# The recurrence of block 2: the two heads of a pair in opposite halves of the array

## The chip, the core and the metric

The kernel runs on one core of a Trainium2 chip. The metric is the device time of one execution in microseconds. Five engines work beside each other: TensorE (PE in the profile, its weight loads PEld), VectorE (DVE), ScalarE (ACT), GpSimd (POOL) and SyncE (SP), which issues most DMAs. TensorE's 128x128 array is addressed by rows (the partitions of the two operands) and columns (the partitions of the output in PSUM), so that a matmul with 64 partitions in and 64 out uses one corner of it.

## The reference

Two blocks of two layers each over 512 tokens and 1024 channels. The change lies in the mixer of the second block, an RWKV-7 time mix with 8 heads of 64 channels:

```
for l in range(2):                                   # second block
    h = rms_norm(x) * (1 + sc1) + sh1
    p = h @ w_in                                     # r, k, v, low ranks, pool features, gates
    ps = z + (prev(z) - z) * mu                      # token shift, z = shifted part of p
    decay, a, g = functions of low-rank products
    kk = k * k_k / ||k * k_k||;  k = k * (1 + (a - 1) * k_a)
    # per head and token:  S = S (diag(w) - kk^T (a kk)) + v k^T ;  y = S r
    y = group_norm(y) * lnx_g + lnx_b + (sum r k r_k) v;  y_a = y * g
    y_b = (trailing means over 2, 4, 8, 16 frames - frame) @ pool_w * pool_scale
    x = x + gt1 * ((gate0 * (y_a @ proj_a) + gate1 * (y_b @ proj_b)) @ w_out)
    x = x + gt2 * ffn(x)
```

## The kernel before

**Projections.** Activations lie with channels on partitions, tokens along the free axis (128 x 512 tiles). A projection (lin_steps, L474) forms an output of 128 channels from 8 input tiles; weights and inputs are split into a high and a low part, so each input tile costs three matmuls with 512 columns (L490). Weight units come by DMA on SP's queue (`raw`); ScalarE casts the high part (`wh`, L432) and VectorE, or GpSimd where `fine` is given, subtracts to get the low part (`wl`, L433). With `fine=2` the generator yields after each two input tiles, that is after six matmuls: a step.

**Interleaving.** `together` takes several generators in turn, one step each; `lent(gen, n)` lends n steps of one. The order so written is a priority: the framework plans each engine's own order from it with its cost model, and adds the semaphores. Pools have fixed numbers of buffers; PSUM has two banks for `lin`, three for `ch` and three for `T2`.

**The mixer of block 2 (mix2, L1306).** First the low-rank features (2s), then k and r (2k, 2r), beside which Rwkv.prep makes, for each of four pairs of heads, the scaled keys `bk` and the queries `ar`: the log decay, its sum over each chunk of 64 tokens, the norm of the keys (n2, an rsqrt on VectorE, spread over channels by the transposes Rn) and the products. Then the following steps, in chunks of 64 tokens, 8 per layer, two chunks to a pair:

- `invert` forms for each chunk and head the 128x128 product of keys and queries (`am`, L1620), masks it (`ah`, L1623), gathers all the 32x32 diagonal blocks in one tile (L1625), and inverts them all by 30 dependent rounds of products and sums on VectorE (L1639, L1642). Beside it runs the projection of v (2v), whose evacuation shifts v and adds the bonus (L1599).
- `ready(Q)` puts the inverses back (L1659), makes the off-diagonal block (px, p2) and the transposed, decayed keys (b2 on ScalarE, bt by transposes).
- `chain(Q)` is the recurrence for two chunks one after the other: R = queries times the state plus the part within the chunk (L1713, L1717), up = the inverse times R (L1728), sn = the state's increment (L1738), yp = the output (L1752, L1756), at the end group norm and transposes back. Both heads of a pair use the same rows and the same columns of the array in R and up; the state is a block-diagonal 128x128 tile per pair, so products with it have 128 rows.

Steps of the pool branch (2p) and of a gate (2g1) fill up: 16 steps of 2v beside `invert`, then 5 and 3 around the first `ready`, 12 beside each of the first three pairs of chunks; the last pair runs beside the projection 2pr1. After it come the other gate, 2pr0 and 2out, and the feed-forward part.

Of the kernel before, what the change touches and what calls it, by code (L numbers as in the profile page):

```python
# [16 lines left out]
S = 512  # L17
# [293 lines left out]
def kernel(ctx: ExitStack, tc: tile.TileContext, aps: dict, out: bass.AP, taps=None, stop=None,  # L311
# [162 lines left out]
    def lin_steps(key, mts, hs, evac, first=0, last=0, tag="lin", fine=0):  # L474
# [8 lines left out]
        def fetch(m, tag):  # L483
            if m // gm not in units:
                units[m // gm] = wunit(key, m // gm, tag, G.tensor_tensor if fine or begun and m < 2 else None)
# [117 lines left out]
    def rms_finish(sl, twice=False):  # L603
# [3 lines left out]
        for t in range(4 if twice else 2):  # L607
            o = sl.start + t % 2 * 128
            mm = T.matmul(ms[:, t:t + 1], sums[t // 2][:, o:o + 128], C("ones", 0, 1), start=True, stop=True)
# [696 lines left out]
    def mix2(l):  # L1306
# [22 lines left out]
        ss, rr, kf = [], [], []  # L1329
        lin_fm(("2s", l), 3, hs, shift_ev(ss, 12, "ss", "f"), first=3)  # L1330
# [5 lines left out]
        wsm = {}  # L1336
# [23 lines left out]
        def kr():  # L1360
            wsm.update({n: small(n, l, "f") for n in ("wa2", "gv")})
            yield from lin_steps(("2k", l), 4, hs, shift_ev(kf, 4, "kf", "f"), fine=2)
            yield from lin_steps(("2r", l), 4, hs, shift_ev(rr, 0, "rr", "f"), fine=2)
# [8 lines left out]
        yb = []  # L1372

        def ev_p(g, ps):
            win = PW[g]
            z = U("z", "v")
            A.copy(z, ps)
            cs = U("cs", "v")
# [7 lines left out]
            def project():  # L1386
                p2 = MX("p2")
                T.matmul(p2, pwt[:, g * 128:g * 128 + 128], d, start=True, stop=True)
                t = U("yb2", "f")
                A.copy(t, p2)  # L1390
                yb.append(t)

            soon.append(project)
# [6 lines left out]
        def ev_g1(m, ps):  # L1400
            gt1.append(U("gt1", "bk"))
# [6 lines left out]
        def beside():  # L1408
            yield from lin_steps(("2p", l), 4, hs, ev_p, fine=2)
            tap(f"2yb{l}", yb)  # L1410
            for n, st in enumerate(lin_steps(("2g1", l), 8, hs, ev_g1, fine=2)):
                yield
                if n % 2 and len(yhl1) < 4 <= n // 6:
                    i = len(yhl1)
                    yhl1.append(split(yb[i], "y", "f", psc[:, i:i + 1]))
# [5 lines left out]
        fill = beside()  # L1421
# [7 lines left out]
        run_soon()  # L1429
# [6 lines left out]
        together(rw.chain(NQ - 1), lin_steps(("2pr1", l), 8, yhl1, ev_b1, fine=2))  # L1436
# [33 lines left out]
        def halve(m):  # L1470
            mhl.append(split(merged[m], "m", "bk", 0.5, "ar"))
# [29 lines left out]
    class Rwkv:  # L1501
# [3 lines left out]
        def __init__(self, l, ss, rr, kf, vf, y, lora, hb):  # L1505
# [7 lines left out]
            self.AH, self.BKT = {}, {}  # L1513
            self.st = None

        def prep(self, p):

            l, ss, kf, lora, hb, NC = self.l, self.ss, self.kf, self.lora, self.hb, self.NC
            ps = lora("wup", ss[0], p)
# [4 lines left out]
            V.tensor_tensor_scan(Lc, C("cs"), lw, 0.0, op0=ALU.mult, op1=ALU.add)  # L1524
            yield
            ps = lora("aup", ss[0], p)
            a = U("a", "f")
            A.activation(a, ps, ACTF.Tanh, bias=hb[:, 4 + p:5 + p], scale=0.5)
# [10 lines left out]
            yield  # L1539
            yield  # L1540
            rb = U("rnb", "f", (128, 8, 64))
            A.copy(rb, rn.unsqueeze(2).to_broadcast([128, 8, 64]))
            yield
# [20 lines left out]
            for q in range(2):  # L1564
                hs_ = slice(q * 256, q * 256 + 256)
                bk = U("bk", "bk", (128, 4, 2, 64))
                V.scalar_tensor_tensor(bk[:, :, 0], c4(a[:, hs_]), 0.5, c4(Wi[:, hs_]), op0=ALU.mult, op1=ALU.mult)
                V.tensor_mul(bk[:, :, 1], c4(k2[:, hs_]), c4(Wi[:, hs_]))
# [14 lines left out]
        def bonus(self, p):  # L1583

            l, vf = self.l, self.vf
            bp = MX("bp", "ch")
            T.matmul(bp, C("bones"), self.rr[p], start=True, stop=True)
            if l:
# [5 lines left out]
                V.tensor_sub(dv, dv, vf[p])  # L1594
# [4 lines left out]
            V.tensor_mul(self.y[p], vf[p], bp)  # L1599
            A.activation(self.y[p], self.y[p], ACTF.Identity, bias=VC("lb", l)[:, p:p + 1])  # L1600

        def begin(self):

            self.sbd = [t.rearrange("p (q h v) -> p q h v", q=4, h=2) for t in sums]
            self.swd = U("swd", "f", (128, 4, 64))
            for t in self.sbd:
                G.memset(t.rearrange("p q h v -> p (q h v)"), 0.0)

        def invert(self):

# [4 lines left out]
            for c in range(NC):  # L1615
                for h in range(2):
                    am = c4(MX("am", "T2"))
                    r = slice(64 * h, 64 * h + 64)
                    for p in range(4):
                        T.matmul(am[:, p], BK[2 * p + c // 4][r, c % 4].rearrange("p s t -> p (s t)"),  # L1620
                                 AR[2 * p + c // 4][r, c % 4].rearrange("p s t -> p (s t)"), start=True, stop=True)
                    ah = self.AH[c, h] = U("ah", "f", (128, 4, 128))
                    V.tensor_mul(ah, am, msk("mA"))  # L1623
                    for e in range(2):
                        A.activation(src[64 * h + 32 * e:64 * h + 32 * e + 32, :, 4 * c:4 * c + 4],  # L1625
                                     ah[32 * e:32 * e + 32, :, 32 * e:32 * e + 32].rearrange("s p t -> s t p"),
                                     ACTF.Copy, scale=-1.0)
# [19 lines left out]
        def ready(self, Q):  # L1647

            BK, wc = self.BK, self.wc
# [3 lines left out]
            up, lo = slice(0, 32), slice(32, 64)  # L1653
            four = [(2 * e + h, self.AH[2 * Q + e, h]) for e in range(2) for h in range(2)]
            for n, (i, ah) in enumerate(four):
                c, h = 2 * Q + n // 2, n % 2
                for e in range(2):
                    cp_ = (A.copy, V.tensor_copy, G.tensor_copy)[(2 * n + e) % 3]
                    cp_(ah[32 * e:32 * e + 32, :, 32 * e:32 * e + 32].rearrange("s p t -> s t p"),  # L1659
                        self.inv[64 * h + 32 * e:64 * h + 32 * e + 32, :, 4 * c:4 * c + 4])  # L1660
            yield
            for i, ah in four:
                V.transpose(tn[up, 4 * i:4 * i + 4], ah[up, :, up])
            yield
            for i, ah in four:
                for p in range(4):
                    T.matmul(px[lo, 4 * i + p], ah[up, p, lo], tn[up, 4 * i + p], start=True, stop=True)  # L1667
            A.copy(X[lo], px[lo])
            yield
            for e in range(2):  # L1670
                c = 2 * Q + e
                bt = c4(MX("bt", "T2"))
                b2 = U("b2", "f", (128, 4, 128))
# [10 lines left out]
            for i, ah in four:  # L1684
                for p in range(4):
                    T.matmul(p2[up, 4 * i + p], X[lo, 4 * i + p], ah[lo, p, lo], start=True, stop=True)  # L1686
# [168 lines left out]
```

## Time and profile before

| | us |
|---|---|
| median of 3 runs | 3695.94 (3693.49 to 3697.94) |
| profiled execution, its own time | 3699.74 |
| its span, first to last instruction | 3697.9 |
| PE busy | 3612.5 (98%) |
| DVE busy | 2129.7 (58%) |
| ACT busy | 1501.6 (41%) |
| POOL busy | 719.2 (19%) |

Ends of matmuls are modelled and consecutive ones overlap in the records, so the cadence is read from start to start. Layer 0 of block 2 runs from about 2040 us, layer 1 from about 2860. The granted clock is TensorE's, 1 for 2.4 GHz; the other level is 1.2 GHz.

### The profile page before, as it was taken

What the parts mean: (1) busy time and instruction counts of PE and PEld (TensorE: products, weight loads), DVE (VectorE), ACT (ScalarE), POOL (GpSimd) and SP (SyncE); (2) the same over time, 40 slices, a digit from 0 to 9 for tenths busy, and PEclk for the clock granted to TensorE, in tenths of its full rate; (3) what the DMA queues carried; (4) which work ended last, traced back from release to release, by engine and by line L of the source; (5) the groups of instructions that cost most, each with busy time, mean ns of one, the idle gap of its engine ahead of it and who ended that gap; (6) DMA issues with size and microseconds to landing.
All of it is one profiled execution on the core that took longest, in us unless ns stands there. A gap on an engine that the chain in (4) does not pass through costs nothing. (4 is left out here: it accounts for less than half of the span.)

```text
span 3697.9 us, 48423 instructions
## 1 busy us (share of the span) xinstructions
PE 3612.5 (98%) x17936; PEld 2856.9 (77%) x17936; DVE 2129.7 (58%) x4610; ACT 1501.6 (41%) x2850; POOL 719.2 (19%) x589
## 2 busy tenths in 40 slices
PE   7999999999999999999999889999999999999998
PEld 6667789888876677898888767788888667788887
DVE  6854536667668555366766873364445773363445
ACT  4565524333345545343334553333233543343233
POOL 3523311000044233110000431320000421320000
PEclk9999999999999999999999999999999989999999
DMA  4212322455422123225553221222223111322222
GB/s 136 88 46 69 101 93 98 154 166 188 143 89 84 45 69 103 97 92 165 178 169 132 80 66 41 90 97 92 91 97 114 66 52 41 96 91 97 91 97 75
DMA packets 124894, 367.60 MB, mean 99 GB/s; under 512 B 14704, under 2 KB 19056, under 8 KB 124656
## 3 DMA queue, kind: packets, MB, share of 16 engines
q1 hardware_dynamic: 119264, 357.15, 29.3%
q10 hardware_dynamic: 5392, 7.35, 0.8%
q8 instruction: 141, 2.31, 0.3%
q14 instruction: 97, 0.79, 0.1%
HBM read 350.28 MB, written 7.34 MB: 97 GB/s over the span
## 5 line engine op out<-in xcount | busy, mean ns | idle before, releaser
L432 ACT CAST wh<-raw 128x512 fp32r<-128x512 f32 x1096 | 670.2, 619 | 1532.7 <-PE lnt L490 1444.3
L490 PE MATMUL lnt<-hH,wh 128*128 128x512 f32 (+1 forms) x3184 | 1267.2, 399 | 10.2 <-DVE x L1321 7.2
L490 PE MATMUL lnt<-hL,wh 128*128 128x512 f32 (+1 forms) x3184 | 1233.5, 388 | 2.2 <-DVE hL L643 2.2
L490 PE MATMUL lnt<-hH,wl 128*128 128x512 f32 (+1 forms) x3184 | 1231.2, 387 | 0.0
L433 DVE TENSOR_TENSOR wl<-raw,wh 128x512 fp32r<-128x512 f32 x772 | 537.1, 704 | 643.4 <-ACT wh L432 640.6
L433 POOL TENSOR_TENSOR wl<-raw,wh 128x512 fp32r<-128x512 f32 x324 | 441.8, 1367 | 1601.5 <-ACT wh L432 1568.0
L490 PEld LDWEIGHTS lnt<-hH,wh 128*128 128x128 f32 x3184 | 604.2, 190 | 184.3 <-issue 47.9
L490 PEld LDWEIGHTS lnt<-hL,wh 128*128 128x128 f32 x3184 | 605.8, 190 | 131.0 <-issue 11.5
L490 PEld LDWEIGHTS lnt<-hH,wl 128*128 128x128 f32 x3184 | 604.9, 190 | 130.5 <-issue 3.2
L490 PE MATMUL lnt<-fH,wh 128*128 128x512 f32 (+1 forms) x864 | 313.9, 364 | 0.0
L490 PE MATMUL lnt<-fL,wh 128*128 128x512 f32 (+1 forms) x864 | 313.2, 363 | 0.1
L490 PE MATMUL lnt<-fH,wl 128*128 128x512 f32 (+1 forms) x864 | 312.7, 362 | 0.0
L490 PEld LDWEIGHTS lnt<-fL,wh 128*128 128x128 f32 x864 | 163.2, 189 | 28.5 <-DVE fL L408 0.5
L490 PEld LDWEIGHTS lnt<-fH,wh 128*128 128x128 f32 x864 | 163.2, 189 | 28.2
L490 PEld LDWEIGHTS lnt<-fH,wl 128*128 128x128 f32 x864 | 163.2, 189 | 27.7
L590 POOL TENSOR_TENSOR sums<-sums,sq 128x256 f32<-128x256 f32 (+1 forms) x61 | 53.4, 881 | 563.3 <-ACT sq L588 562.1
L1300 DVE SCALAR_TENSOR_TENSOR x<-lnt,mod,x 128x512 f32<-128x512 f32 (+1 forms) x136 | 88.7, 655 | 92.1 <-PE lnt L490 91.9
L695 DVE SCALAR_TENSOR_TENSOR cv<-lnt,vec,cv 128x511 f32<-128x511 f32 (+1 forms) x168 | 123.9, 744 | 14.7 <-ACT cv L693 13.2
L490 PE MATMUL lnt<-yH,wh 128*128 128x512 f32 x320 | 129.9, 406 | 0.0
L490 PE MATMUL lnt<-yH,wl 128*128 128x512 f32 x320 | 127.6, 399 | 0.0
L490 PE MATMUL lnt<-yL,wh 128*128 128x512 f32 x320 | 126.4, 395 | 0.0
L1281 DVE CUSTOM_DVE_ANT_0 adaw<-adaw,csilu 128x512 f32<-128x512 f32 x192 | 124.5, 685 | 0.0
(389 smaller groups left out, 4330.6 us busy)
## 6 DMA issues: line engine op xcount, KB each, us to landing
raw<-in_wst_dram SPq DMA_DIRECT2D x548, 512.0 KB, 3.3
adaw<-in_ada_dram SPq DMA_DIRECT2D x192, 256.0 KB, 3.5
sw<-rq ACTq DMA_DIRECT2D x96, 64.0 KB, 2.0
xd<-x SPq DMA_DIRECT2D x16, 256.0 KB, 2.5
x<-xd SPq DMA_DIRECT2D x16, 256.0 KB, 3.3
x<-in_xT_dram SPq DMA_DIRECT2D x8, 256.0 KB, 5.8
out_dram<-x SPq DMA_DIRECT2D x8, 256.0 KB, 2.2
csilu<-in_c_dram SPq DMA_DIRECT2D x4, 256.0 KB, 4.4
```

What stands on the lines that cost most here:

```text
L432: A.copy(h[:, :q], raw[:, sl])
L433: sub(l[:, :q], raw[:, sl], h[:, :q].bitcast(F32), op=ALU.subtract)
L490: mm = T.matmul(ps[:, sl], w_, h_[:, sl], start=(k == 0 and i == 0), stop=(k == kt - 1 and i == 2))
L590: G.tensor_tensor(acc[:, sl], acc[:, sl], sq[:, sl], op=ALU.add)
L695: V.scalar_tensor_tensor(y[:, d:], ps[:, :S - d], taps_w[nt - 1 - d], y[:, d:], op0=ALU.mult, op1=ALU.add)
L1281: V.tensor_tensor_reduce(out=w, in0=w, in1=t, scale=1.0, scalar=0.0, op0=ALU.mult, op1=ALU.add, accum_out=sm[:, i:i + 1])
L1300: return V.scalar_tensor_tensor(x[m][:, sl], ps[:, sl], md[:, o + m:o + m + 1], x[m][:, sl], op0=ALU.mult, op1=ALU.add)
```

## The change

In `invert` the am products of two heads alternate and go to two banks. In `ready` each head's blocks stay in its own half of the partitions, and the keys are transposed without the decay. In `chain` the state has no zero halves (128 x 4 x 64), R and up run with head 0 in one half of rows and columns and head 1 in the other, R's part within the chunk is formed for both chunks ahead (R1), the decay is multiplied into the state after the sum, and y is formed for both chunks at the end, into one bank per head. The last transposes and the addition to y become `tail`, which runs beside the next pair. The evacuation of v and the bonus moves from VectorE to ScalarE (both scalings, the copy of the bonus) and GpSimd (sum, products). 2v, 2p and 2g1 become one filler; 31 of its steps run beside `invert`, 5 beside the first `ready`, 9 beside each pair. The pool branch's scan and product come later by a count of matmuls. Besides: the two low-rank products of prep are issued together, the rsqrt of the norms gets more rounds, half of bk goes to GpSimd, the k, r and v projections take banks of `lin` and `T2` in turn, two small weights are fetched earlier, and in rms_finish the sum-of-squares matmuls are tied behind the last projection matmul. The cut core of the diff (of `chain` mainly the new lines):

```diff
 def fetch(m, tag):            # lin_steps
-  ... G.tensor_tensor if fine or begun and m < 2 else None)
+  ... G.tensor_tensor if fine else None)
-            ps = MX("lnt", tag)
+            ps = MX("lnt", tag if isinstance(tag, str) else tag[m % len(tag)])
...
+        with behind() if newest else ExitStack():          # rms_finish
             for t in range(4 if twice else 2):
                 mm = T.matmul(ms[:, t:t + 1], sums[t // 2][:, o:o + 128], C("ones", 0, 1), start=True, stop=True)
...
+        begun.append(smalls)                               # mix2
         lin_fm(("2s", l), 3, hs, shift_ev(ss, 12, "ss", "f"), first=3)
...
+            banks = ("lin", "lin", "T2")
+            yield from lin_steps(("2k", l), 4, hs, shift_ev(kf, 4, "kf", "f"), tag=banks, fine=2)
+            yield from lin_steps(("2r", l), 4, hs, shift_ev(rr, 0, "rr", "f"), tag=banks, fine=2)
...
         def ev_vf(m, ps):
-            shift(vf[m], ps, 8 + m)
+            A.activation(vf[m], ps, ACTF.Identity, bias=0.0, scale=om[:, 8 + m:9 + m])
+            A.activation(t, ps, ACTF.Identity, bias=0.0, scale=mu[:, 8 + m:9 + m])
+            G.tensor_tensor(vf[m][:, 1:], vf[m][:, 1:], t[:, :S - 1], op=ALU.add)
...
+            later.append([20, lambda: pool(g)])            # ev_p
...
+            later.insert(0, [14, project])                 # pool
...
         def beside():
+            yield from lin_steps(("2v", l), 4, hs, ev_vf, tag=("lin", "T2"), fine=2)
             yield from lin_steps(("2p", l), 4, hs, ev_p, fine=2)
...
-        together(rw.invert(), lin_steps(("2v", l), 4, hs, ev_vf, fine=2))
+        together(rw.invert(), lent(fill, 31))
...
-        for _ in lent(fill, 5):
-            pass
-        together(rw.ready(0), lent(fill, 3))
+        together(rw.ready(0), lent(fill, 5))
         for Q in range(NQ - 1):
-            together(rw.chain(Q), rw.ready(Q + 1), lent(fill, 12))
+            together(tails(), rw.chain(Q), rw.ready(Q + 1), lent(fill, 9))
...
+            ps, ps2 = lora("wup", ss[0], p), lora("aup", ss[0], p)      # prep
...
-            yield
-            yield
+            for _ in range(3):
+                yield
             rb = U("rnb", "f", (128, 8, 64))
             A.copy(rb, rn.unsqueeze(2).to_broadcast([128, 8, 64]))
+            yield
             yield
...
-                V.scalar_tensor_tensor(bk[:, :, 0], c4(a[:, hs_]), 0.5, c4(Wi[:, hs_]), op0=ALU.mult, op1=ALU.mult)
-                V.tensor_mul(bk[:, :, 1], c4(k2[:, hs_]), c4(Wi[:, hs_]))
+                for h in range(2):
+                    r = slice(64 * h, 64 * h + 64)
+                    V.scalar_tensor_tensor(bk[r, :, h], c4(a[r, hs_]), 0.5, c4(Wi[r, hs_]), op0=ALU.mult, op1=ALU.mult)
+                    G.tensor_tensor(bk[r, :, 1 - h], c4(k2[r, hs_]), c4(Wi[r, hs_]), op=ALU.mult)
...
+            A.copy(y[p], bp)                                # bonus
-                V.tensor_sub(dv, dv, vf[p])
+                G.tensor_tensor(dv, dv, vf[p], op=ALU.subtract)
-            V.tensor_mul(self.y[p], vf[p], bp)
+            G.tensor_tensor(y[p], y[p], vf[p], op=ALU.mult)
...
-            for t in self.sbd:                              # begin
-                G.memset(t.rearrange("p q h v -> p (q h v)"), 0.0)
...
+                ams = [c4(MX("am", "T2")) for _ in range(2)]            # invert
+                for p in range(4):
+                    for h in range(2):
+                        r = slice(64 * h, 64 * h + 64)
+                        T.matmul(ams[h][:, p], BK[2 * p + c // 4][r, c % 4].rearrange("p s t -> p (s t)"),
+                                 AR[2 * p + c // 4][r, c % 4].rearrange("p s t -> p (s t)"), start=True, stop=True)
...
-                    A.activation(b2[:, p], BK[2 * p + c // 4][:, c % 4].rearrange("p s t -> p (s t)"), ACTF.Copy,
-                                 scale=wc[:, c, p:p + 1])               # ready
-                    T.transpose(bt[:, p], b2[:, p], ident)
+                    T.transpose(bt[:, p], BK[2 * p + c // 4][:, c % 4].rearrange("p s t -> p (s t)"), ident)
...
+            R = MX("R1", "ch").rearrange("p (e q v) -> p e q v", e=2, q=4)   # chain
+            for e in range(2):
+                for p in range(4):
+                    for h in range(2):
+                        T.matmul(R[half[h], e, p], AH[2 * Q + e, h][half[1 - h], p, 0:64], uvs[e][half[1 - h], p, h], ...)
+            A.activation(Rv, R, ACTF.Copy, scale=-1.0)
+            for e in range(2):
+                if st is not None:
+                    for p in range(4):
+                        for h in range(2):
+                            T.matmul(R[half[h], p], AR[2 * p + q][half[h], cc, 0], st[half[h], p], start=True, stop=True)
+                    V.scalar_tensor_tensor(Rs, R, -1.0, Rs, op0=ALU.mult, op1=ALU.add)
+                for p in range(4):
+                    for h in range(2):
+                        T.matmul(up_[half[h], p], AH[c, h][half[h], p, 0:64], Rs[half[h], p], start=True, stop=True)
+                A.copy(uv[half[0], :, 0], up_[half[0]])
+                V.tensor_copy(uv[half[1], :, 1], up_[half[1]])
+                if c < NC - 1:
+                    for p in range(4):
+                        for h in range(2):
+                            T.matmul(sn[half[h], p], BKT[p, c][:, half[h]], uv[:, p, h], start=True, stop=True)
+                    V.tensor_add(new, sn, st)
+                    V.tensor_mul(new, new, w_)
+            yps = [MX("yp", "ch").rearrange("p (i q v) -> p i q v", i=2, q=4) for _ in range(2)]
+            for p in range(4):
+                for h, e in ((0, 0), (1, 1), (0, 1), (1, 0)):
+                    T.matmul(yps[h][half[e], 0, p], AR[2 * p + c // 4][half[h], c % 4, 1], olds[e][half[h], p], ...)
+            for p in range(4):
+                for h in range(2):
+                    for e in range(2):
+                        T.matmul(yps[h][half[e], 1, p], AH[2 * Q + e, h][:, p, 64:128], uvs[e][:, p, h], ...)
...
```

## Rows read from the trace of the kernel before

**Rows 1.** The page's first part: busy us, share of the span, instructions.
```profile
PE 3612.5 (98%) x17936; PEld 2856.9 (77%) x17936; DVE 2129.7 (58%) x4610; ACT 1501.6 (41%) x2850; POOL 719.2 (19%) x589
```

**Rows 2.** Stage table: length, busy us per engine, granted clock, DMA share, GB/s.
```profile
2100.00:2135.00 35.00, 30.32 (x117) 22.25 (x117) 30.43 (x60) 15.37 (x27) 19.53 (x16) 0.90 0.17 59
2157.00:2196.00 39.00, 30.11 (x111) 21.94 (x110) 38.71 (x139) 15.01 (x30) 20.82 (x19) 0.91 0.25 81
2196.00:2330.00 134.00, 130.62 (x1042) 98.79 (x1041) 54.58 (x176) 53.54 (x124) 27.65 (x22) 0.93 0.14 47
2915.00:2955.00 40.00, 34.04 (x146) 24.99 (x146) 33.62 (x66) 16.33 (x28) 21.13 (x17) 0.91 0.20 70
2977.00:3019.00 42.00, 34.66 (x121) 23.29 (x119) 41.84 (x126) 14.95 (x27) 17.68 (x13) 0.92 0.24 82
3019.00:3156.00 137.00, 132.30 (x1019) 98.69 (x1020) 54.26 (x178) 53.50 (x126) 27.51 (x27) 0.89 0.13 41
```

**Rows 3.** Waits of PE, 2050 to 2420 (layer 0): us, times, longest.
```profile
PE p L1388 <- ACT wh L432: 6.8, 1, 6.8
PE Rn L1546 <- ACT rnb L1542: 4.7, 2, 2.5
```

**Rows 4.** Timeline of PE in a recurrence of layer 0: start, us, instruction, count.
```profile
2211.65 0.69 PE L1667 MATMUL px<-tn,ah 32*32 32x32 f32 x16
2212.27 0.49 PE L490 MATMUL lnt<-hH,wl 128*128 128x512 f32 x1
2212.69 1.14 PE L1717 MATMUL R<-uv,ah 64*64 64x64 f32 x16
2213.77 0.69 PE L1667 MATMUL px<-tn,ah 32*32 32x32 f32 x16
...
2218.33 0.69 PE L1738 MATMUL sn<-uv,bkt 128*64 128x64 f32 x16
2218.95 0.55 PE L1677 MATMUL bt<-cst,b 128*128 128x128 f32 x3
...
2226.97 0.43 PE L1713 MATMUL R<-sums,ar 128*64 128x128 f32 x2
...
2229.90 0.50 PE L490 MATMUL lnt<-hH,wh 128*128 128x512 f32 x1
...
2230.47 0.40 PE L490 MATMUL lnt<-hH,wl 128*128 128x512 f32 x1
2230.70 0.40 PE L490 MATMUL lnt<-hH,wh 128*128 128x512 f32 x1
...
2231.50 1.14 PE L1728 MATMUL up<-Rs,ah 64*64 64x64 f32 x16
2232.57 0.50 PE L490 MATMUL lnt<-hH,wh 128*128 128x512 f32 x1
...
2237.66 0.43 PE L1752 MATMUL yp<-sums,ar 128*64 128x128 f32 x2
...
2239.61 0.50 PE L490 MATMUL lnt<-hH,wh 128*128 128x512 f32 x1
```

**Rows 5.** The same view, at the am products of layer 0.
```profile
2144.38 3.10 PE L1620 MATMUL am<-ar,bk 64*128 64x128 f32 x32
2147.40 0.49 PE L490 MATMUL lnt<-hH,wh 128*128 128x512 f32 x1
```

**Rows 6.** Timelines of POOL and DVE late in the inversion of layer 0.
```profile
2183.63 2.52 POOL L433 TENSOR_TENSOR wl<-raw,wh 128x512 fp32r<-128x512 f32 x2 [6.71 <-ACT wh L432]
2183.70 2.50 DVE L1639 TENSOR_TENSOR tm<-sums 128x56 f32<-128x56 f32 x2
2186.13 0.30 DVE L1642 TENSOR_TENSOR sums<-sums,tm 128x56 f32<-128x56 f32 x2
```

**Rows 7.** Groups by line: count, busy us, mean ns, idle before (whole span; 2150 to 2720).
```profile
L1342 PE MATMUL lo<-ss,sm_wa 64*128 64x512 f32 x32 | 17.9, 640 | 0.0
...
L1762 DVE TENSOR_TENSOR swd<-sums,wc 64x256 f32<-64x256 f32 x12 | 5.4, 447 | 0.3
```

More of the change, by code (lines that the diff above doesn't have):

```diff
@@ L484, in fetch @@
             if m // gm not in units:
-                units[m // gm] = wunit(key, m // gm, tag, G.tensor_tensor if fine or begun and m < 2 else None)
+                units[m // gm] = wunit(key, m // gm, tag, G.tensor_tensor if fine else None)
         def part(m, ps, sl, k):
@@ L606, in rms_finish @@
         ms = MX("ms", first_of("pb", "ch", "nm"))
-        for t in range(4 if twice else 2):
-            o = sl.start + t % 2 * 128
-            mm = T.matmul(ms[:, t:t + 1], sums[t // 2][:, o:o + 128], C("ones", 0, 1), start=True, stop=True)
+        with behind() if newest else ExitStack():
+            for t in range(4 if twice else 2):
+                o = sl.start + t % 2 * 128
+                mm = T.matmul(ms[:, t:t + 1], sums[t // 2][:, o:o + 128], C("ones", 0, 1), start=True, stop=True)
         newest[:] = [mm.ins]
@@ L1329, in mix2, with smalls @@
         ss, rr, kf = [], [], []
+        wsm = {}
+        def smalls():
+            wsm.update({n: small(n, l, "f") for n in ("wa2", "gv")})
+        begun.append(smalls)
         lin_fm(("2s", l), 3, hs, shift_ev(ss, 12, "ss", "f"), first=3)
@@ L1683, in ready @@
             p2 = MX("p2", "T2").rearrange("p (q c) -> p q c", q=16)
-            for i, ah in four:
-                for p in range(4):
-                    T.matmul(p2[up, 4 * i + p], X[lo, 4 * i + p], ah[lo, p, lo], start=True, stop=True)
-            for i, ah in four:
-                A.activation(ah[up, :, lo], p2[up, 4 * i:4 * i + 4], ACTF.Copy, scale=-1.0)
+            for p in range(4):
+                for i, up, lo, ah in four:
+                    T.matmul(p2[up, 4 * i + p], X[lo, 4 * i + p], ah[lo, p, 32:64], start=True, stop=True)
@@ new lines, in chain @@
+            yield
+            R = MX("R1", "ch").rearrange("p (e q v) -> p e q v", e=2, q=4)
+            for e in range(2):
+                for p in range(4):
+                    for h in range(2):
+                        T.matmul(R[half[h], e, p], AH[2 * Q + e, h][half[1 - h], p, 0:64], uvs[e][half[1 - h], p, h],
+                                 start=True, stop=True)
+            Rv = U("Rv", "f", (128, 2, 4, 64))
+            A.activation(Rv, R, ACTF.Copy, scale=-1.0)
+            yield
@@ new lines, in chain @@
+            yn = U("yn", "f", (128, 4, 2, 64))
+            for h in range(2):
+                r = slice(0, 128)
+                if olds[0] is None:
+                    A.copy(yn[half[0], :, h], yps[h][half[0], 1])
+                    r = half[1]
+                A.copy(yn[r, :, h], yps[h][r, 1])
+                V.tensor_add(yn[r, :, h], yn[r, :, h], yps[h][r, 0])
+            yield
+            bs = SM("gst", 48, 2).rearrange("p (q h c) -> p q h c", q=4, h=2)
+            mv = SM("gmv", 16, 2).rearrange("p (q h c) -> p q h c", q=4, h=2)
@@ new lines, in chain @@
+            for h in range(2):
+                for p in range(4):
+                    V.bn_stats(bs[:, p, h], yn[:, p, h])
+                    V.bn_aggr(mv[:, p, h], bs[:, p, h])
+            vv = SM("gvv", 8, 2)
+            V.tensor_scalar(vv.rearrange("p (q h) -> p q h", q=4), mv[:, :, :, 1], EPS_GN, None, op0=ALU.add)
+            rs = rsqrt(vv, 8, "gn")
+            for h in range(2):
+                V.tensor_sub(yn[:, :, h], yn[:, :, h], mv[:, :, h, 0:1].to_broadcast([128, 4, 64]))
+            yn = yn.rearrange("p q h v -> p (q h) v")
@@ L1788, with tail @@
+            if Q < NC // 2 - 1:
+                self.tails.append(tail)
+            else:
+                for _ in range(3):
+                    yield
+                tail()
+        def tail(self):
+            while self.tails:
+                self.tails.pop(0)()
     try:
@@ L1829 @@
         for l in range(DEPTH):
[L1830 removed]
+            with phase(dict(bk0=4, bk1=4, ar=8, room=1, f=33), dict(lin=2, ch=3, T2=3)):
                 mix2(l)
```

223 lines of the change are left out of this document (89 added, 134 removed).

## The prediction

> **What bounds the kernel now.** I read the page first. TensorE (PE) is busy for 98% of the span [rows 1], so time can only be won where PE works badly, stands still, or runs at the lower of its two clock levels. The stage table of block 2's mixer [rows 2] shows where. In the two stretches where the chunk matrices are inverted (2157 to 2196 in layer 0, 2977 to 3019 in layer 1) VectorE is busy 38.71 of 39 us and 41.84 of 42, PE only 30.11 and 34.66: there VectorE sets the pace, and PE stands still for 8.9 + 7.3 = 16.2 us. The waits name it: PE waits 6.8 us at one place for a weight cast that comes only after the inversion, and 4.7 us in each layer for the key norms to be spread (Rn) [rows 3]. In the two stretches of the recurrence (134 and 137 us) PE hardly stands still, but the timeline shows small matmuls back to back for about half of the time [rows 4]; there the cost is the cadence of the small passes, and the clock (0.93 and 0.89 granted).
>
> **Cadence of the small passes.** One fp32 matmul is two passes in the trace. From one start to the next group's start [rows 4]: 16 passes of R without a state take 2213.77 - 2212.69 = 1.08 us, 16 of up 1.07 us: 67 ns each, all in one 64x64 corner. The 16 passes of sn, whose heads go to alternate column halves, take 0.62 us: 39 ns each, with the same 64 columns moving. R with a state mixes two shapes: 2.93 us for its 24 passes; y with a state 1.95 us for 24. A projection matmul with 512 columns takes 0.23 us.
>
> **The change, part by part.** *Recurrence.* Per chunk with a state, before: 2.93 (R) + 1.07 (up) + 1.95 (y) = 5.95 us. After: R1 16 passes (64x64, half of a pair's 32), R on the state 16, up 16, y on the state 16, y on the values 16 = 80 passes, each followed by one in another half of the rows or columns. If these go as sn does, 80 x 39 ns = 3.12 us: 2.83 us less. If nothing overlaps, 80 x 67 = 5.36 us: 0.59 less. A layer has 7 such chunks and one without a state (before 1.08 + 1.07 + 1.07, taking its y like up; after 48 x 39 ns = 1.87, or 48 x 67 = 3.22). Sum of two layers: 2 x (7 x 2.83 + 1.35) = 42.3 us, or 2 x 7 x 0.59 = 8.3 us. I take 42.3, because sn is the nearest row: alternate halves, the same 64 columns. If two corners also multiply at the same moment a pass could cost half of 39 ns: 80 x 16 x 19.5 ns = 25 us more.
> The Trainium skill ("TensorEngine Tiling (Array Packing)", Restrictions and Gotchas) says that different row tiles cannot use one PSUM bank at the same moment. The two heads of R1, R and up are different row tiles writing two halves of one bank; no row of before shows such a pair. By that rule these 48 of the 80 passes would stay at 67 ns and the recurrence would give 22 us, 2 x (7 x 1.49 + 0.45), instead of 42.3.
>
> *am.* 32 passes take 2147.40 - 2144.38 = 3.02 us, 94 ns each [rows 5]; a layer has 128. The change alternates row halves into two banks. Scaled as sn to up (39/67): 55 ns, 39 ns x 256 = 10 us. Bounds: nothing, and half of the time, 12 us. px and p2 are 32x32 and already at 39 ns (0.62 us for 16 [rows 4]); I take nothing for them. The two lora products, put side by side in opposite row halves, cost 17.9 us busy in all [rows 7] and could give at most a quarter of that, 4 us, as only their second passes could go beside the first; I take nothing.
>
> *Inversion.* 31 steps of projection now run from its start, where 16 did, and 5 more beside the first ready. A step is 6 matmuls, 1.4 us, so 15 steps are 21 us of work that doesn't wait for VectorE; they come out of what follows (27 steps beside the first three pairs of chunks instead of 36). VectorE loses the shift of v and the product with the bonus; ScalarE gets two passes of v and a copy of the bonus, and has 15 of 39 us busy there, so this hides. GpSimd gets the additions and products. Of the 16.2 us idle I take half, 8 us (bounds 0 to 16), since the added GpSimd work slows VectorE (below).
>
> *Rn.* Two more rounds ahead of the spread and one after it give VectorE's rsqrt its time; of 4.7 us in each layer I take half, 4.7 in all (0 to 9.4). Next late is bk, where half of the products go to GpSimd.
>
> *Clock.* Lost to the lower level (1.2 GHz), by length x (1 - granted): 134 x 0.07 + 137 x 0.11 + 39 x 0.09 + 42 x 0.08 + 35 x 0.10 + 40 x 0.09 = 38.5 us [rows 2]. Each fall follows idle time of PE or a stretch of small passes; both shrink, neither goes. I take half, 19 us (0 to 38).
>
> *At nothing.* The b scaling that goes from ScalarE, the two memsets, the scan and differences of the pool branch (same work, later) lie beside PE work. The state update now has its product with the decay behind the sum, on the path from chunk to chunk: some 0.45 us, as a product of that length takes [rows 7], 14 times, 6 us if uncovered; one projection step of 1.4 us stands beside each round and covers it. The projections of k, r and v borrow a PSUM bank of the am tiles, so that am can wait for its mask product; the projections go on meanwhile. The two small weights are fetched between the first weight units on SP's queue; what is queued behind them is the third unit, not used until two outputs are done. The sum-of-squares matmuls are tied behind the last projection on PE; VectorE's rsqrt waits for them, and 8 norms could lose or win 0.5 us each: -4 to +4.
>
> **Sum.** 42.3 + 10 + 8 + 4.7 + 19 = 84 us. The profiled execution takes 3699.7 us (span 3697.9), so 3615.7; it lies 3.8 above the median of the three runs, so the forecast is 3612.
>
> **Rivals.**
> *A: the passes don't overlap.* Two row halves that write one bank may have to go in turn, as all 64-row passes of before do. Then the recurrence gives 8.3 and am nothing: 44 us less gain, 3656. For it: no row shows two row halves overlapping. Against it: sn overlaps within one bank. This is also the case in which the change doesn't do what it says, and the skill's rule above stands on this side. The same skill's "TensorE: Matmul & The Clock Gate" (Part 3: Packing small matmuls) has tiles in different rows and columns run at once, which would give the 25 us more.
> *B: GpSimd holds VectorE up.* Two casts' differences on GpSimd take 2.52 us, and in just that time two VectorE products of the inversion take 2.50 [rows 6], where two sums of the same size after it take 0.30. In the inversion the change adds per layer 8 GpSimd passes (sum of v, product of the bonus), 4 more in layer 1, and the differences of 3 more weight units (6): 32 passes in all x 1.26 = 40 us. If VectorE loses all of it and PE runs out of the moved steps, the gain falls by 40: 3652. If the bk products (32, half as long) hold it too, by 60: 3672. Against it: PE has 21 us more to do per layer.
> *C: slower, by the clock.* The recurrence already falls to the lower level, with PE 97% busy by the records. If packed passes count for less, it stays there. The work in the two stretches is 271 us less 25 lost to the clock, less 42 of passes and 9 projection steps per layer (2 x 13), so about 178 us at full speed; at the lower level throughout it loses 178 instead of the 12 that I leave: +166, 3778. It is slower than before once 96 of these 178 us, some 54%, run low (today 25 of 246, 10%). Against it: the share of projections among this work doesn't fall.
>
> **Chances.** Forecast 0.58, A 0.16, B 0.18, C 0.05, nothing measurable 0.03. A difference of 0.2%, 7 us, is about what a measurement here can tell. The range goes from 3562 (all idle, wait and clock terms back, half of the 25) to 3670 (B's far end); C and what lies lower are left out. Faster 0.91, same 0.03, slower 0.06.
>
> **What would show it.** R, up and y groups of 16 passes at 0.6 us instead of 1.07, am's 32 at 1.8; in the inversion PE over 36 of 39 us busy; clock in the recurrence over 0.95; Rn without a wait. It is wrong if R's passes stay at 67 ns (A), if the inversion's products show more stretches like that of 2.50 us and PE waits behind them (B), or if the granted clock in the recurrence falls under 0.8 (C).

## The result and the profile after

| kernel | median us | runs | ratio to before, 95% interval |
|---|---|---|---|
| before | 3694.72 | 3693.14 to 3697.94 | |
| changed | 3646.90 | 3642.74 to 3652.54 | 0.9869 [0.9854, 0.9884] |

The change is worth 47.8 us, 1.3%, where 84 were forecast. The profiled execution of the changed kernel takes 3652.54 us (span 3650.1), so the two traces differ by 47.8 us as well and can be set against each other; both lie some 5 us above their kernel's median. The page's first part, beside [rows 1]:

```profile
PE 3537.1 (97%) x18160; PEld 2806.6 (77%) x18160; DVE 2160.7 (59%) x4586; ACT 1503.1 (41%) x2838; POOL 776.8 (21%) x637
```

PE has 75 us less to do, but the span fell by 48 only. The stage table says where; the stretches are the preparation, the inversion (two rows) and the recurrence of layer 0, then the later part of the inversion and the recurrence of layer 1 (columns as in [rows 2]; the inversion is wider than there, since the first px now comes later):

```profile
2100.00:2135.00 35.00, 29.74 (x116) 22.59 (x112) 31.50 (x50) 15.46 (x28) 31.03 (x29) 0.82 0.16 52
2135.00:2165.00 30.00, 23.80 (x159) 18.81 (x159) 20.13 (x31) 15.99 (x37) 6.86 (x6) 0.83 0.16 55
2165.00:2226.00 61.00, 46.54 (x207) 35.49 (x207) 56.24 (x153) 24.68 (x47) 35.90 (x31) 0.86 0.23 78
2226.00:2306.00 80.00, 79.16 (x1007) 60.23 (x1002) 33.70 (x115) 41.52 (x91) 19.41 (x16) 1.00 0.15 49
2953.00:3021.00 68.00, 54.20 (x195) 37.85 (x194) 67.14 (x160) 27.57 (x52) 46.18 (x35) 0.89 0.21 66
3021.00:3107.00 86.00, 85.13 (x1010) 64.61 (x1012) 34.13 (x116) 41.63 (x91) 19.23 (x15) 0.92 0.14 45
```

The recurrence, counted from the first px to the last transposed output, went from 167.3 and 171.2 us to 113.4 and 119.8 and runs at full clock in layer 0. The inversion, from the first am to the first px, went from 62.6 and 69.7 us to 90.5 and 97.0; of these 28 and 27 us more, 14 and 11 are projections that moved there (198 matmuls of 0.23 us in each, 138 and 149 before). In the third row PE stands still for 14.5 of the 61 us, and the clock of the inversions is at 0.83 to 0.89. The waits of PE, first layer 0 (2073 to 2450), then layer 1 (2862 to 3141), beside [rows 3]:

```profile
PE lnt L490 <- ACT yb L1386: 14.5, 1, 14.5
PE n L1554 <- ACT ksq L1550: 6.7, 2, 5.3
PE am L1642 <- DVE ar L1603: 6.0, 1, 6.0
...
PE lo L1348 <- ACT x L1611: 7.4, 1, 7.4
PE n L1554 <- ACT ksq L1550: 6.0, 2, 4.6
PE am L1642 <- DVE ar L1603: 5.7, 1, 5.7
PE lnt L490 <- ACT yb L1386: 4.3, 1, 4.3
```

Before, am waited 0.3 us in all and the other three not at all. Rn's wait is nearly gone (1.7 us in all), but its place is taken by n, the sum of squares ahead of it, which is now issued before ScalarE has squared k. The am tiles wait for ar. The longest wait is for a PSUM bank that ScalarE (yb) was to empty. ScalarE's waits from 2180 to 2215 show why it was late:

```profile
ACT ah L1682 <- DVE room L1668: 16.1, 1, 16.1
```

The copies of the inverted blocks stand ahead of yb in ScalarE's queue, and they need the end of VectorE's inversion. VectorE is held up in turn. POOL and DVE late in the inversion of layer 0, beside [rows 6] (start, us, instruction, count):

```profile
2183.74 4.77 POOL L433 TENSOR_TENSOR wl<-raw,wh 128x512 fp32r<-128x512 f32 x2 [1.34 <-PE bp L1610]
...
2185.60 0.47 DVE L1665 TENSOR_TENSOR sums<-sums,tm 128x126 f32<-128x126 f32 x2
2185.99 2.66 DVE L1662 TENSOR_TENSOR tm<-sums 128x120 f32<-128x120 f32 x2
2188.57 1.56 DVE L1665 TENSOR_TENSOR sums<-sums,tm 128x120 f32<-128x120 f32 x2
```

Two products that have just taken 0.47 us take 2.66 while GpSimd works. In the single records of the trace, which the timeline merges into rows, each of them lasts 1.37 us, as long as the GpSimd pass beside it (1.33). The first of GpSimd's differences takes 3.48, and for its first 2.2 us VectorE's products beside it go at their 0.26 to 0.28: either engine can be the one that is held up.

In layer 1 it is GpSimd that is held up most, and ScalarE stands behind it (its waits from 2940 to 3021, then one product on GpSimd):

```profile
ACT x L1624 <- POOL x L1623: 25.6, 4, 12.1
...
2976.54 4.72 POOL L1623 TENSOR_TENSOR x<-x,x 128x512 f32<-128x512 f32 x1 [5.83 <-DVE x L1620]
```

The copy of the bonus for which PE waits 7.4 us (x L1611) stands next but one behind that wait in ScalarE's queue. VectorE's rounds themselves, from the first product to the last, take 34.3 us in layer 0 and 40.0 in layer 1; before they took 30.9 and 41.9.

**The passes.** PE in the recurrence of layer 0, beside [rows 4]:

```profile
2247.94 0.40 PE L490 MATMUL lnt<-hH,wl 128*128 128x512 f32 x1
2248.27 0.68 PE L1759 MATMUL up<-Rv,ah 64*64 64x64 f32 x16
2248.88 0.50 PE L490 MATMUL lnt<-hH,wh 128*128 128x512 f32 x1
...
2252.68 0.68 PE L1783 MATMUL yp<-sums,ar 64*64 64x64 f32 x16
2253.29 1.15 PE L1788 MATMUL yp<-uv,ah 128*64 128x64 f32 x32
2254.37 0.50 PE L490 MATMUL lnt<-hH,wh 128*128 128x512 f32 x1
...
2260.05 1.15 PE L1739 MATMUL R<-uv,ah 64*64 64x64 f32 x32
2261.13 0.69 PE L1689 MATMUL px<-tn,ah 32*32 32x32 f32 x32
2261.75 0.50 PE L490 MATMUL lnt<-hH,wh 128*128 128x512 f32 x1
```

From start to next start: up's 16 passes 0.61 us, y on the state 0.61, R1's 32 passes 1.08 (34 ns each), px's 32 in 0.62 (19 ns; before, 16 took that long). The single records show the pattern. In one corner (up before) a pass starts 58 ns after the last. Where two corners alternate (up, R1), two passes start 7 ns apart and each such pair 58 ns after the last. Where four alternate (y on the state, from a layer's second pair of chunks on), four start within 20 ns, and each four again 58 ns after the last.

The am products, beside [rows 5], take 3.02 us for 32 as before:

```profile
2154.21 3.10 PE L1642 MATMUL am<-ar,bk 64*128 64x128 f32 x32
2157.23 0.49 PE L490 MATMUL lnt<-hH,wh 128*128 128x512 f32 x1
```

That is no steady pace. The first 16 passes do go side by side: two starts 7 ns apart, each pair 112 ns after the last, 1.00 us in all. Then passes follow singly every 112 ns, and after the sixth none starts for 0.39 us. The weight loads go on when VectorE's mask product of an earlier am tile has ended (at 2156.09 in the single records), which frees a PSUM bank; there are three, and two are now taken at once:

```profile
2154.21 1.63 PEld L1642 LDWEIGHTS am<-ar,bk 64*128 64x128 f32 x22 [0.37 <-DVE ah L1646]
2156.15 0.96 PEld L1642 LDWEIGHTS am<-ar,bk 64*128 64x128 f32 x10 [0.31 <-DVE ah L1646]
...
2155.40 1.29 DVE L1646 TENSOR_TENSOR ah<-am,cst 128x512 f32<-128x512 f32 x2 [1.36 <-PE am L1642]
```

In the trace of before, one head's passes start 112 ns apart as well, and the first ones of the next head already run beside the last ones of it (starts 4 to 6 ns apart, in two banks).

The two lora products of a row block, four passes in opposite row halves, now take 1.06 us:

```profile
2073.34 1.13 PE L1348 MATMUL lo<-ss,sm_wa 64*128 64x512 f32 x4
2074.40 0.50 PE L490 MATMUL lnt<-hH,wh 128*128 128x512 f32 x1
```

In the trace of before two passes alone take as long:

```profile
2074.76 1.12 PE L1342 MATMUL lo<-ss,sm_wa 64*128 64x512 f32 x2
2075.81 0.50 PE L490 MATMUL lnt<-hH,wh 128*128 128x512 f32 x1
```

**One account for all kernels.** Of each trace I took all PE rows from the first lora product to the last output projection in both layers, gave each the time up to the next one's start, and counted what lies between an end and the next start as idle. "Low" is the part of the busy time at the lower clock level; half of it is lost.

| us, two layers | busy | of it low | idle | sum | busy at full clock |
|---|---|---|---|---|---|
| before | 798.4 | 75.5 | 35.4 | 833.8 | 760.6 |
| changed | 723.2 | 63.2 | 63.1 | 786.3 | 691.6 |
| v on VectorE | 716.0 | 45.4 | 47.2 | 763.2 | 693.3 |
| bk on VectorE | 716.2 | 47.8 | 57.0 | 773.2 | 692.3 |
| v and bk | 716.0 | 46.1 | 45.0 | 761.0 | 693.0 |
| recurrence alone | 721.4 | 34.9 | 41.8 | 763.2 | 704.0 |
| preparation's rounds | 710.6 | 30.0 | 44.7 | 755.3 | 695.6 |

From before to changed: work at full clock -69.0, clock -6.1, idle +27.7, together -47.5 of the 47.8 us. So the change saved more work than forecast, and gave 28 us back as idle.

### The profile page after: what moved, and what is told of

It is laid out like the page before. It is cut to its first block, busy times and chain, and to the rows that moved or that the text cites. A ratio compares the mean times of both kernels' runs of the same rounds, so it can differ in the third digit from the quotient of the medians.

```text
span 3650.1 us, 48877 instructions
## 1 busy us (share of the span) xinstructions
PE 3537.1 (97%) x18160; PEld 2806.6 (77%) x18160; DVE 2160.7 (59%) x4586; ACT 1503.1 (41%) x2838; POOL 776.8 (21%) x637
## 4 chain that ended last, share of the span: by engine, by line
PE 87%; DVE 9%; ACT 2%; issue 1%; DMA 1%; POOL 0%; SPq 0%; DVEq 0%; ACTq 0%; POOLq 0%
PE lnt L490 77%; PE at L845 1%; PE pv L868 1%; DVE tm L1662 1%; PE lnt L548 1%; DVE sums L1665 1%; DVE bk L1590 1%; PE am L1642 1%; DVE wl L433 1%; DVE hn L634 1%; PE tp L861 1%; PE sp L941 0%; PE is L819 0%; ACT wh L432 0%; DVE hL L644 0%
## 5 line engine op out<-in xcount | busy, mean ns | idle before, releaser
L490 PEld LDWEIGHTS lnt<-fH,wl 128*128 128x128 f32 x864 | 163.0, 189 | 27.7
```

What stands on the lines that cost most here:

```text
L490: mm = T.matmul(ps[:, sl], w_, h_[:, sl], start=(k == 0 and i == 0), stop=(k == kt - 1 and i == 2))
```

## Experiments

All were timed beside the kernel before on the same chip; ratios are to it.

**Heads in turn** (R1, R and up without the alternation).

```diff
-                for p in range(4):
-                    for h in range(2):
+                for h in range(2):
+                    for p in range(4):
                         T.matmul(R[half[h], e, p], AH...
```

> The changed kernel, but R1, R and up run all four pairs of head 0 and then all four of head 1, so that neighbouring passes share their corner of the array. Theory (alternating halves make the passes overlap): these three groups go from 34 to 44 ns a pass back to about 67; 48 passes a chunk x 16 chunks x 30 ns = 23 us slower than the changed kernel, about 3670. Rival (the gain is from the 64x64 state in place of a 128x128 one that mixed two shapes): the passes stay under 45 ns and the time within 5 us of 3647.

3659.99 us, ratio 0.9893 [0.9877, 0.9909]: by the ratios 9 us, by the account above 10.5 us lost of what was won, less than half of what was expected. Its R1 and up:

```profile
2260.51 1.54 PE L1739 MATMUL R<-uv,ah 64*64 64x64 f32 x32
2261.98 0.69 PE L1689 MATMUL px<-tn,ah 32*32 32x32 f32 x32
...
2267.51 0.96 PE L1759 MATMUL up<-Rv,ah 64*64 64x64 f32 x16
2268.40 0.66 PE L1697 MATMUL bt<-cst,bk 128*128 128x128 f32 x4
```

R1's 32 passes take 1.47 us (46 ns) and up's 16 take 0.89 (56 ns), against 1.08 and 0.61. So passes of two row halves that write one bank do overlap, and rival A falls. 56 ns is less than the 67 of before [rows 4], though, and the single records of up show why: within a head the passes start 58 ns apart, as before, but the second head's first pass starts 6 ns after the first head's fifth. The two heads still overlap where one follows the other.

**Block copies on VectorE** (all 32 of a layer; none on ScalarE or GpSimd).

```diff
-                    cp_ = (A.copy, V.tensor_copy, G.tensor_copy)[(2 * n + e) % 3]
+                    cp_ = V.tensor_copy
```

> The changed kernel, but the 32 copies a layer that put the inverted blocks back all run on VectorE (a third each on ScalarE, VectorE, GpSimd before). Theory (ScalarE stands at the first of these copies until the inversion ends, and the evacuations and weight casts behind it starve PE): the wait of PE for the evacuation of 2p, 14.5 us in layer 0 and 4.3 in layer 1, goes; 5 to 20 us faster, 3627 to 3642. Rival (VectorE's late inversion itself is what PE waits for): the idle time moves to px, and the copies, all on one engine, add some 5 us a layer: 3647 to 3657.

3653.80 us, 0.9883 [0.9869, 0.9898]: no faster. The 14.5 us wait goes and others come in its place (by the same account 69.0 us idle). That copies block ScalarE's queue is where the idle shows, not what causes it.

**v on VectorE** (its shift, the difference and the bonus product).

```diff
-            A.activation(vf[m], ps, ACTF.Identity, bias=0.0, scale=om[:, 8 + m:9 + m])
-            A.activation(t, ps, ACTF.Identity, bias=0.0, scale=mu[:, 8 + m:9 + m])
-            G.tensor_tensor(vf[m][:, 1:], vf[m][:, 1:], t[:, :S - 1], op=ALU.add)
+            shift(vf[m], ps, 8 + m)
...
-            G.tensor_tensor(y[p], y[p], vf[p], op=ALU.mult)
+            V.tensor_mul(y[p], vf[p], bp)
```

> The changed kernel, but the shift of v, the difference for layer 1 and the product of the bonus are done on VectorE from PSUM, as in the kernel before. Theory (GpSimd's passes hold up VectorE's rounds of the inversion and, through the chain of v, ScalarE's queue): VectorE gets 6 to 8 us more to do a layer and loses 8 to 12 blocks of up to 1.3 us; the inversion ends some 5 to 8 us earlier and layer 1's wait of PE for the bonus (7.4 us) goes: 3627 to 3640. Rival (it is well that PSUM is emptied by ScalarE, VectorE being the late engine): 5 to 15 us slower, 3652 to 3662.

3631.61 us, 0.9821 [0.9807, 0.9836]: 0.48% or 17 us faster than the changed kernel. From the first am to the first px 81.5 and 88.4 us instead of 90.5 and 97.0. Its PE waits:

```profile
PE n L1551 <- ACT ksq L1547: 13.5, 4, 5.3
PE am L1638 <- DVE ar L1600: 12.1, 2, 6.3
...
PE lnt L490 <- ACT yb L1383: 9.6, 3, 4.5
```

The 14.5 is down to 4.5 and the 7.4 of layer 1 is gone; am's wait stays. VectorE's rounds take 30.9 and 39.2 us again. The edit takes work from GpSimd and from ScalarE at once, so it does not tell the two apart.

**bk on VectorE** (the half of the bk products that GpSimd got).

```diff
-                    G.tensor_tensor(bk[r, :, 1 - h], c4(k2[r, hs_]), c4(Wi[r, hs_]), op=ALU.mult)
+                    V.tensor_mul(bk[r, :, 1 - h], c4(k2[r, hs_]), c4(Wi[r, hs_]))
```

> The changed kernel with the second half of the bk products back on VectorE (v's shift and the block copies stay as changed). Theory: the GpSimd half of bk is what makes the am tiles wait for ar (6.0 and 5.7 us), and TensorE's clock falls right behind that wait; so the wait goes and the time falls by 8 to 18 us against the changed kernel (ratio to before 0.982 to 0.985). Rival: VectorE itself is late there, with or without GpSimd's half, so the wait stays near 6 us per layer and the time within 4 us of the changed kernel (ratio 0.986 to 0.988).

3636.65 us, 0.9846 [0.9832, 0.9859], some 8 us faster than the changed kernel. Its waits:

```profile
PE lnt L490 <- ACT yb L1386: 19.1, 2, 14.4
...
PE am L1642 <- DVE ar L1603: 8.8, 2, 4.4
```

am's wait falls from 11.7 to 8.8 us in all and the idle by 6; most of that wait stays, so GpSimd's half of bk makes a part of it only.

**Both.** The two diffs together.

> v's shift and bonus product and the second half of bk all back on VectorE; everything else as changed. Theory (GpSimd's work holds VectorE up and stretches the way to the inversion): the 17 us measured for v alone and the 8 to 18 expected for bk alone add, as they sit in different stretches: ratio to before 0.977 to 0.980. Rival (VectorE is simply full there): little more than v alone, 0.981 to 0.983.

3627.02 us, 0.9819 [0.9805, 0.9833]: no different from v alone. The rival holds: the gains do not add in the medians, though the profiled executions differ by 2 us in the account.

**am in turn** (the kernel above, with am's order and single banks of before).

```diff
-                ams = [c4(MX("am", "T2")) for _ in range(2)]
-                for p in range(4):
-                    for h in range(2):
+                for h in range(2):
+                    am = c4(MX("am", "T2"))
...
+                    for p in range(4):
...
```

> The kernel with v and bk on VectorE, and the am tiles computed as before: one row half after the other, a PSUM bank each, masked as soon as one is done. Theory: am's passes take 94 ns in either order, so the alternation gains nothing, and taking two banks at once before either can be masked makes the am stage longer; with the old order the am stage shrinks by 4 to 8 us in each layer and the time by 5 to 14 us against v and bk on VectorE alone. Rival: the am stage is long because of the waits for its inputs and not for the banks; then the time stays within 4 us.

3625.02 us, 0.9813 [0.9800, 0.9827], and the am stage as long (24.3 us in each layer): the order of am neither gains nor costs anything that the times can tell. That the two banks make the stage longer was wrong.

**Recurrence alone** (the new recurrence, am and bk's new layout; preparation, evacuation of v and distribution of the projection steps as before; the earlier fetch of two small weights and the tied sum-of-squares matmuls stay in).

```diff
-        together(rw.invert(), lent(fill, 31))
+        together(rw.invert(), lin_steps(("2v", l), 4, hs, ev_vf, fine=2))
...
-            together(tails(), rw.chain(Q), rw.ready(Q + 1), lent(fill, 9))
+            together(tails(), rw.chain(Q), rw.ready(Q + 1), lent(fill, 12))
```

> The new recurrence (am, ready, chain, state, y, tail) with the preparation, the evacuation of v and the distribution of the projection steps of the kernel before (16 of 2v beside the inversion, 5 and 3, then 12 a pair). Theory (the recurrence gains some 39 us a layer, and the rest of the change loses it in part in the inversion, 13 us a layer): 3695 - 78 = 3617, and up to 3630 if some of the gain hangs on the schedule. Rival (the gain of the recurrence comes from the moved steps): 3650 to 3670.

3625.12 us, 0.9803 [0.9786, 0.9819]: 72 us faster than before and by the ratios 24 faster than the whole change. With am's order put back as well:

> The new recurrence alone (preparation, evacuation and distribution of steps of before; measured 72 us faster than before), now with am's order of before too. Theory: its stretch from the first am to the first px is 6.5 us longer in each layer than before (69.3 and 76.0 against 62.6 and 69.7), by the pair of banks that am takes; with the old order it is as before, and the time falls by 8 to 14 us: ratio to before 0.976 to 0.978. Rival: the block copies or the later start cause it; no change, 0.979 to 0.981.

3627.42 us, 0.9820 [0.9807, 0.9833]: no gain here either (by the ratios 6 us slower, with overlapping intervals); its stretch from the first am to the first px stays at 70.1 and 77.4 us.

**Lora products in pairs**, the one edit of the preparation added to the recurrence alone.

```diff
-            ps = lora("wup", ss[0], p)
+            ps, ps2 = lora("wup", ss[0], p), lora("aup", ss[0], p)
...
```

> The new recurrence alone (72 us faster than before), with the two lora products of a row block issued together from opposite halves of the rows, as in the change. Theory: the pair multiplies side by side; from the occupancy in the traces (0.53 us a matmul alone, 0.27 in a pair, 32 of 40 matmuls in a pair) this is worth 8 us: ratio to before 0.977 to 0.9785. Rival: TensorE then only waits 8 us longer for the key norms in the same stretch; no change, 0.9795 to 0.982.

3623.01 us, 0.9793 [0.9780, 0.9806]: between the two expectations, not told apart. A gain up to some 8 us is not excluded. By the account, the profiled execution has 9.2 us less work at full clock and 3.8 less idle than the recurrence alone, and loses 7.9 more to the lower clock.

**Steps ahead of am** (v and bk on VectorE).

```diff
-        together(rw.invert(), lent(fill, 31))
+        for _ in lent(fill, 4):
+            pass
+        together(rw.invert(), lent(fill, 27))
```

> The kernel with v and bk on VectorE, and four of the 31 projection steps issued before the first am tile instead of beside the inversion. Theory: TensorE stands 4.4 us in each layer in front of the first am (for ar), and its clock falls right behind that; 24 matmuls of 0.23 us (5.6 us) placed there cover the wait, so that idle and low clock of the stretch shrink by 4.4 + up to 3.4 us in each layer: 8 to 14 us faster than v and bk on VectorE alone, ratio to before 0.978 to 0.980. Rival: the inversion starts later by what is put before it, and runs out of steps at its end by as much; the idle only moves, and the time stays within 4 us (0.981 to 0.983).

3627.45 us, 0.9809 [0.9795, 0.9822]: nothing. am's waits go down to 2.5 and 2.1 us, 2.0 and 1.2 of them for a bank that VectorE's mask product frees. PE stands for 10.9 at the end of layer 0's inversion instead: the rival.

**The preparation's rounds as before**, on top of that.

```diff
             A.activation(lw, ps, ACTF.Tanh, bias=hb[:, p:p + 1], scale=0.5)
...
+            yield
             a = U("a", "f")
...
-            yield
             kcol = VC("kk", l)[:, p:p + 1]
...
-            for _ in range(3):
-                yield
+            yield
+            yield
...
-            yield
...
```

> As the kernel with the steps ahead of am, with the rounds of the preparation's steps put as before (one more ahead of the key norms' sums, two fewer behind them), the lora products still in pairs. Theory: TensorE's wait of 5.7 and 1.4 us in each layer for the squares of k (no such wait before) is what the earlier norm sums cost; it goes and Rn's 4.7 us a layer comes back, so little is won: within 5 us of the kernel with the steps ahead. Rival: with VectorE unloaded both waits go, 8 to 14 us faster.

3619.69 us, 0.9787 [0.9773, 0.9800]: the lowest median of the study, under before and the changed one, and 7.8 us under the one it was built on, on the same chip: past the theory's 5 and just short of the rival's 8. am's wait goes, n's falls to 2.4 us in each layer, Rn's comes back (6.7 in all). By the account the time at the low clock, half of which is lost, shrinks from 43.1 to 30.0 us and the idle from 48.0 to 44.7. What is left:

```profile
PE p L1399 <- ACT yb L1383: 10.9, 1, 10.9
...
PE Rn L1564 <- ACT rnb L1560: 6.7, 3, 3.0
PE px L1686 <- DVE tn L1682: 6.7, 1, 6.7
```

**The pooled product later.** An attempt on the 10.9.

```diff
-            later.append([20, lambda: pool(g)])
+            later.append([8 if g else 56, lambda: pool(g)])
```

> The kernel with the steps ahead and the preparation's rounds as before, and the first pooled product set back by 36 matmuls of projection (the later ones 12 apart less, so that the last stands where it did). Theory: the 10.9 us for which TensorE stands at the end of layer 0's inversion, and the 2.5 us in layer 1, are one wait for that product, whose difference VectorE makes only after the inversion; with 5.6 to 8.4 us of projections in front of it most of that goes: 6 to 11 us faster, ratio to before 0.9755 to 0.977. Rival: what stands behind it (px, which needs the inverted blocks themselves) is as late, and the idle moves there; within 3 us, 0.978 to 0.980.

3629.34 us, 0.9820 [0.9806, 0.9833]: 12 us slower by the ratios than without it, so neither expectation held; by the account the idle grows by 3.9 us and the loss to the clock by 5.2. Its waits:

```profile
PE px L1686 <- DVE tn L1682: 15.3, 2, 10.7
...
PE lnt L490 <- ACT yb L1383: 9.3, 3, 6.5
```

The wait moved to px, which needs the inverted blocks: the end of VectorE's inversion is what PE waits for, whatever stands first in its queue.

## Why the prediction was too low by 35 us

*Recurrence: -42.3 forecast, -47.9 found.* At full clock R, up, y and sn take 51.6 us in the two layers instead of 99.5. The step was right: the passes go as sn did (38 ns for up, 34 for R1), those of y on the state at 38 ns where 16 stand together and at 19 where 32 do (six of the eight groups: 0.62 us). The 5.6 us more come mostly from four corners running at once in y on the state, the forecast's case of half the 39 ns, for these passes alone. Rival A is shown wrong: over both layers the passes of R1, R and up, which alternate two row halves within one bank, take 32 to 46 ns on average, and 48 to 56 without the alternation. The rule of the Trainium skill that stood behind it ("TensorEngine Tiling (Array Packing)", Restrictions and Gotchas) does not hold for these passes; the measurement decides.

*am: -10 forecast, -0.2 found.* The scaled pace, 55 ns, is there, 56 ns in the first half of a group of 32, but the term was not. First, 94 ns was no pace of passes in turn: within one head it is 112, and neighbouring heads overlapped already, so "as all 64-row passes of before do" was wrong. Second, a pair of heads holds two of three banks, and the second half of a group stands until VectorE's mask product frees one. That the banks are the cause is read from the trace; the runs with single banks are as fast, but they have no more overlap either.

*Taken at nothing: -15.5 found.* px and p2 fell by 7.0 us, the lora products by 8.5. I bounded the lora at 4, as if only second passes could overlap; the rows show the whole pair at once, 1.06 us for both. Here the Trainium skill's "TensorE: Matmul & The Clock Gate" (Part 3: Packing small matmuls) agrees: products in different rows run together. Another 5.4 us are small products and projections that follow on them.

*Inversion and Rn: -8 and -4.7 forecast, +27.7 found.* This is the step that failed. I let 15 moved steps buy half of PE's idle time; but PE takes its work in order, and each moved step needs a cast, a difference and an emptied bank, from the very engines to which the change gave more. Undoing GpSimd's new work (v and bk) takes 18.1 us of idle and 8.6 of clock out of the account; the medians give 18 us. Rival B's mechanism, VectorE held up, did act, beside the forecast: of the rounds' products and sums in the two layers, 30 last over 0.7 us, 16 before and 13 with v moved back. At some 1.1 us each that is 15 us more than before, where 40 to 60 had been priced. As VectorE was spared the work on v, its rounds are only 3.4 us longer in layer 0 and 0.8 in layer 1 than with v moved back. For the rest the trace shows GpSimd's passes late in v's own chain, and ScalarE's queue behind them; no run separates the two. It is not all: 10 us of idle more than before stay without that work. Of the waits left there, n's (14.3 us) comes from the new rounds, since it fell to 4.7 with the old ones; those in front of am and px only changed places when work was moved around them.

*Clock: -19 forecast, -6.1 found.* It did rise in the recurrence (from 0.93 to 1.00 in layer 0). It fell in layer 0's preparation and in both inversions, at new waits: 0.82 where PE waits for n, 0.83 at am's wait for ar. In layer 1's preparation n's wait is there too (6.0 us), and the clock is at 0.94. With fewer waits it came back: recurrence alone -20.3 against before, about what I had forecast for the whole. Rival C did not come.

Sum of the terms: -47.9 - 0.2 - 15.5 - 5.4 = -69 work, +27.7 idle, -6.1 clock. Luck has a part in how near the result came: 21 us of it are work that I had put at nothing. Of the signs, the groups of 0.6 us came; am's 1.8 us, PE's 36 of 39 us and, in layer 1, a clock over 0.95 did not. The range's lower end was summed wrong: the parts named for it give some 3567, not 3562. The recurrence alone took 72 us: the forecast's passes and clock, 42.3 + 19, with px and p2's 7.0 beside them, come to 68. The rest of the change as a whole lost some 22 to 24 of them.

## What to carry over

Price a moved step not by the engine that is to be filled but by each engine that has to serve it in that stretch: in the inversion VectorE was busy 38.71 of 39 us [rows 2], and every step put there had to be served past it. When idle time before an engine moves with every rearrangement, look for what ends last (here the inversion on VectorE) and shorten that; no run here did so by itself. And undo parts of a change that is measured as a gain: here one part alone was worth half as much again as the whole.

## What the runs showed of the hardware

- 64x64 passes at full clock, from start to start: in one corner 58 ns (67 a pass over a group of 16, with its first and last pass). With two corners alternating, a pair every 58 ns (38 a pass over 16, up); with four, four every 58 ns (19 a pass over 32, y on the state). In up the two corners write two halves of one bank.
- Two products of 64 rows in opposite row halves, 512 columns moving, into two banks: 1.06 us for both, 1.05 for one alone. With 128 columns moving (am) a pass starts every 112 ns in one row half, a pair every 112 ns in two; 94 ns over a group of 32, since a bank comes free late.
- A VectorE product that meets a GpSimd pass can last as long as it: 1.37 us, where two together have just taken 0.47. It can be the other way about: GpSimd passes of 1.3 us took 3.48 and 4.72 beside VectorE products of 0.25 to 0.29.
